# A gated MLP whose down projection is made from seven products of quadrants instead of the plain blocks

## The chip, the core and the metric

One core of a Trainium2 chip runs the whole layer. Its engines run side by side, each with its own instruction queue: TensorE (PE in the profile, with its weight loads shown apart as PEld), VectorE (DVE), ScalarE (ACT), GpSimd (POOL) and SyncE (SP, which here only issues DMAs). The metric is the device time of one execution in microseconds (us); lower is better.

## The reference, cut to what matters

One layer of a causal decoder over 2048 tokens with D = 1024 channels, in float32: attention in eight heads with three dilations beside pooling groups, then a gated MLP of width 2816 with a causal convolution of width 3, then a gated embedding, then a norm.

```python
h = x
hn = _rmsnorm(h, ln_mix[i])
z = hn @ w_in[i]
...
att = _dilated_attention(q, k, v, slopes)
pool = _multiscale_pool(u, pool_w[i], pool_scale[i])
h = h + jnp.concatenate([att, pool], axis=-1) @ w_out[i]
hn = _rmsnorm(h, ln_ffn[i])
up = _causal_dwconv(hn @ w_up[i], conv_w[i], conv_b[i])
gate, val = jnp.split(up, 2, axis=-1)
h = h + (jax.nn.silu(gate) * val) @ w_down[i]
g = jax.nn.sigmoid(_rmsnorm(h, ln_ple[i]) @ w_ple_gate[i])
h = h + g * (p[i] @ w_ple[i])
return _rmsnorm(h, ln_final)
```

The mixture of dilations in the attention weighs each branch by its softmax statistics (`m` the maximum, `d` the denominator): `w = d * exp(m - max(m))`, normalised over the branches.

## The kernel before

**Tiling.** Channels lie on the 128 partitions, tokens on the free axis. A chunk is 512 tokens (`CH`), and there are four (`NCH`). `KD` = 8 blocks of 128 channels make up D, `NF` = 22 blocks the 2816 of the MLP. Every float32 operand of a product is split into a high part (a cast on ACT, L84) and a low part (a subtraction, L85, on DVE or POOL), and `mm3` (L88) multiplies high by high (L89), high by low (L90) and low by high (L91) into the same bank of PSUM: three matmuls of 128x128 by 128x512 for each block.

**Stages.** The input projection runs to about 399 us, the attention to about 735, the output projection `w_out` to about 940, the up product from 942 to 1780 in two halves of 1024 tokens, the down product from 1782 to about 2293, the gate and the final norm to the end.

**Attention.** A list of stages with lags (`CFG["ord"]`) writes out by hand which step of which head each engine does next. `mix` (L705) counts steps d from the end of a pair of heads. At d = 1 the statistics of the pair go to DRAM (tiles std, stf), at 4 they are loaded back (tiles sn and sf), and the list `CFG["m"]` holds the steps of what follows: `mix_lift` (L858: on DVE the minimum `lo` at L862, two differences, an exponential on ACT), `mix_weights` (L870: five operations on DVE and a store of the weights to DRAM by POOL's queue), then for each chunk c `mix_fetch` (the weights broadcast back by POOL's queue), `mix_products` and `mix_store`, both on POOL. Its first three numbers are the step of the lift, of the weights and of the first fetch, the fourth the distance between chunks, the last two the distances from a fetch to its products and its store. Since DVE does its work in the order in which it is written, whatever stands behind L862 waits with it. DVE also does the maxima of the scores (L577, L583), the low part of the transposed weights (L617) and the sum of two halves (L660, once in two steps).

**Up product.** For each of the 22 blocks f and each half there is one turn. A turn computes gate and value block (256 channels by 1024 tokens) with seven products of quadrants in place of eight: the operands a11, a12, a22, s1 to s4 of the activations (`A`, high and low parts of four tiles each) by b11, b21, t2, t1, t3, t4, b22 of the weights (`product`, L1309, 12 matmuls each, L1315). The sums t1 to t4 of the weights are made on POOL in the first half (L1038 to L1040, L1051), stored to DRAM, and loaded back in the second. DVE splits them (L85, tile wu), adds the products (`add`, L1338), does the convolution (`conv_b`, L1328 to L1335) and the product of gate and value (L1512); ACT does the rest (SiLU, L1502). `after(slot)` is called seven times a turn: in turn 0 and around the change of half, `Refill.take` (L1359) splits operands that came by DMA (its `fetch` keeps `depth` loads ahead, in borrowed tiles of the tags nt, inv and dg; low parts at L1372); from turn 2 on, `prepare` (L1097) makes the operands of the second half piece by piece. In it `spread_prep` (L114) makes two diagonal tiles dg for each chunk (L123), and `spread` (L133) broadcasts the scale of a chunk by two matmuls into a bank bc (L137), which frees those tiles. Each turn ends with one store of 128x1024 activations to DRAM (`g.act`, tile act, L1513).

**Down product.** It runs by chunk c, by block f, by eight blocks j of the output: 4 x 22 x 8 x 3 matmuls into seven banks dn and an eighth, dn7, that runs five blocks later (`wait`). `ahead` and `act_ahead` load (SP) and split, three steps ahead, the weights of f (128x1024, tile rd, L954 and L1544) and the activations of f and c (128x512, tile ra, L1559). Three pairs are prepared during the last turn of up (`first_units`, L1379). `closed` adds the residual h (L1586) and stores h2, and `fin` makes the statistics of the norm some steps later. Five of the eight blocks of the gate's weights follow in the same queue of loads behind the last block of down.

The whole of up is written out by hand (`tc.manual_schedule`): its order in the code is its order on every engine. In the down product a scheduler orders each engine's queue.

## Time and profile before

| what | us |
| --- | --- |
| median of 3 runs (2514.61 to 2520.33) | 2520.25 |
| the profiled execution | 2522.12 |
| its span | 2519.8 |
| PE busy | 2407.5 (96%) |
| DVE busy | 1588.8 (63%) |
| ACT busy | 1108.6 (44%) |
| POOL busy | 515.7 (20%) |

The granted clock of PE in this execution is 0.98 on the mean. The chain that ended last lies on PE for 79% of the span, on DMA and on DVE for 6% each. The longest waits of PE by line are:

```profile
PE o L628 <- DVE s L660: 23.3, 30, 4.8
PE o L642 <- DVE s L660: 14.6, 29, 2.5
PE sn L572 <- DVE st L577: 13.6, 3, 6.4
```

A row of the waits names who waited for whom, then us in total, the number of times and the longest. Here all three are in the attention. A row in order of time gives the start, the duration, the engine, the line, the operation, output <- input, shapes, and in brackets the idle time ahead of it with what ended it. A row of groups gives the count, then busy us and mean ns of one, then idle time with what ended it. A row of a stretch gives busy times in the order PE, PEld, DVE, ACT, POOL. Durations of overlapping matmuls are longer than the distance between their starts.

### The profile page before, as it was taken

What the parts mean: (1) busy time and instruction counts of PE and PEld (TensorE: products, weight loads), DVE (VectorE), ACT (ScalarE), POOL (GpSimd) and SP (SyncE); (2) the same over time, 40 slices, a digit from 0 to 9 for tenths busy, and PEclk for the clock granted to TensorE, in tenths of its full rate; (3) what the DMA queues carried; (4) which work ended last, traced back from release to release, by engine and by line L of the source; (5) the groups of instructions that cost most, each with busy time, mean ns of one, the idle gap of its engine ahead of it and who ended that gap; (6) DMA issues with size and microseconds to landing.
All of it is one profiled execution on the core that took longest, in us unless ns stands there. A gap on an engine that the chain in (4) does not pass through costs nothing.

```text
span 2519.8 us, 31897 instructions
## 1 busy us (share of the span) xinstructions
PE 2407.5 (96%) x11515; PEld 2022.4 (80%) x11515; DVE 1588.8 (63%) x2416; ACT 1108.6 (44%) x1923; POOL 515.7 (20%) x423
## 2 busy tenths in 40 slices
PE   8999998888779999999999999999999999999998
PEld 7888887777767877888887888888788888887888
DVE  6635427777774467888888666666535374435755
ACT  5423326887751135544446444444323242323322
POOL 3312221053430023333340000000122222221000
PEclk9999999999879999999999999999999999999999
DMA  7534358687646674555556334333546464635332
GB/s 240 174 120 180 142 178 248 166 193 180 164 164 221 223 252 167 167 177 181 175 194 211 122 117 138 121 114 117 191 134 222 149 219 150 208 122 173 124 105 88
DMA packets 209052, 424.08 MB, mean 168 GB/s; under 512 B 42464, under 2 KB 68896, under 8 KB 205824
## 3 DMA queue, kind: packets, MB, share of 16 engines
q1 hardware_dynamic: 170576, 368.41, 46.4%
q0 software_dynamic: 18672, 25.88, 3.1%
q10 hardware_dynamic: 19648, 27.77, 3.1%
q8 instruction: 90, 1.47, 0.2%
q14 instruction: 66, 0.54, 0.1%
HBM read 290.01 MB, written 131.89 MB: 167 GB/s over the span
## 4 chain that ended last, share of the span: by engine, by line
PE 79%; DMA 6%; DVE 6%; issue 3%; ACT 2%; POOL 0%; SPq 0%; ACTq 0%; POOLq 0%; DVEq 0%
PE ua L1315 18%; PE uc L1315 9%; PE dn L90 6%; PE dn L91 6%; PE dn L89 6%; PE ub L1315 4%; PE z L91 4%; PE z L89 4%; PE z L90 4%; PE o L89 2%; PE o L91 2%; PE o L90 2%; PE gp L89 2%; PE gp L91 2%; PE gp L90 2%
## 5 line engine op out<-in xcount | busy, mean ns | idle before, releaser
L89 PE MATMUL dn<-ah,hd 128*128 128x512 f32 x704 | 275.3, 391 | 2.8 <-ACT ah L84 2.8
L90 PE MATMUL dn<-al,hd 128*128 128x512 f32 x704 | 274.9, 391 | 1.7 <-DVE al L85 1.7
L91 PE MATMUL dn<-ah,ld 128*128 128x512 f32 x704 | 274.6, 390 | 0.0
L85 POOL TENSOR_TENSOR ld<-rd,hd 128x1024 fp32r<-128x1024 f32 x42 | 100.9, 2403 | 812.8 <-ACT hd L84 812.8
L84 ACT CAST hd<-rd 128x1024 fp32r<-128x1024 f32 x88 | 92.5, 1052 | 266.3 <-PE dn L90 230.9
L85 DVE TENSOR_TENSOR al<-ra,ah 128x512 fp32r<-128x512 f32 x88 | 116.8, 1330 | 136.0 <-ACT ah L84 136.0
L89 PE MATMUL z<-hnh,wh 128*128 128x512 f32 (+1 forms) x480 | 170.3, 355 | 9.9 <-ACT hnh L252 5.8
L90 PE MATMUL z<-hnl,wh 128*128 128x512 f32 (+1 forms) x480 | 170.0, 354 | 2.7 <-DVE hnl L253 2.6
L91 PE MATMUL z<-hnh,wl 128*128 128x512 f32 (+1 forms) x480 | 169.9, 354 | 2.3 <-POOL wl L85 1.7
L89 PEld LDWEIGHTS dn<-ah,hd 128*128 128x128 f32 x704 | 132.7, 188 | 31.0 <-ACT ah L84 3.2
L90 PEld LDWEIGHTS dn<-al,hd 128*128 128x128 f32 x704 | 132.7, 188 | 29.8 <-DVE al L85 2.2
L91 PEld LDWEIGHTS dn<-ah,ld 128*128 128x128 f32 x704 | 132.7, 189 | 27.4
L85 DVE TENSOR_TENSOR wu<-ru,wu 128x1024 fp32r<-128x1024 f32 x88 | 127.4, 1448 | 0.0
L155 DVE TENSOR_TENSOR acc<-acc,sq 128x512 f32<-128x512 f32 (+1 forms) x125 | 90.2, 722 | 47.6 <-ACT sq L154 34.6
L1315 PE MATMUL uc<-a22h,wu 128*128 128x512 f32 x352 | 115.7, 389 | 1.8 <-DVE uv L1338 1.8
L1315 PE MATMUL ua<-s2h,wu 128*128 128x512 f32 x352 | 115.8, 390 | 1.1 <-ACT ug L1452 1.1
L1315 PE MATMUL uc<-s3h,wu 128*128 128x512 f32 x352 | 116.2, 390 | 0.3 <-ACT s3h L1371 0.3
L1315 PE MATMUL ub<-a12h,wu 128*128 128x512 f32 x352 | 115.9, 390 | 0.3 <-ACT a12h L1371 0.3
L1315 PE MATMUL ua<-s4h,wu 128*128 128x512 f32 x352 | 115.5, 389 | 0.0
L1315 PE MATMUL ua<-s1h,wu 128*128 128x512 f32 x352 | 115.5, 389 | 0.0
L1315 PE MATMUL ua<-a11h,wu 128*128 128x512 f32 x352 | 115.5, 389 | 0.0
L85 DVE TENSOR_TENSOR ld<-rd,hd 128x1024 fp32r<-128x1024 f32 x46 | 56.2, 1223 | 89.1 <-ACT hd L84 89.1
(317 smaller groups left out, 6474.4 us busy)
## 6 DMA issues: line engine op xcount, KB each, us to landing
rd<-in_w_down_dram SPq DMA_DIRECT2D x88, 512.0 KB, 3.6
ru<-in_w_up_dram SPq DMA_DIRECT2D x66, 512.0 KB, 4.1
ra<-act SPq DMA_DIRECT2D x88, 256.0 KB, 3.8
act<-yg SPq DMA_DIRECT2D x43, 512.0 KB, 3.1
wr<-in_w_in_dram SPq DMA_DIRECT2D x64, 256.0 KB, 4.0
nt<-h SPq DMA_DIRECT2D x56, 256.0 KB, 3.9
h<-h SPq DMA_DIRECT2D x56, 256.0 KB, 5.6
td<-t SPq DMA_DIRECT2D x22, 512.0 KB, 2.6
```

Of the source, the lines that this page charges most:

```text
L84: nc.scalar.copy(hi, src)
L85: (low or nc.gpsimd).tensor_tensor(lo, src, fp(hi), op=ALU.subtract)
L89: nc.tensor.matmul(ps, wh, ah, start=first, stop=False)
L90: nc.tensor.matmul(ps, wh, al, start=False, stop=False)
L91: nc.tensor.matmul(ps, wl, ah, start=False, stop=last)
L155: nc.vector.tensor_tensor(acc[:, :n], acc[:, :n], sq[:, :n], op=ALU.add)
L1315: nc.tensor.matmul(pst, x[:, ksl], y, start=first and k == 0 and n == 0, stop=k == HK - 1 and n == 2, skip_group_check=True)
```

## The change

Four things change together.

1. **Down product.** It works on two halves of 1024 tokens, on pairs of blocks f = q and q + 11, and on quadrants of 128x512. Seven products (`SEQ`) of 11 steps q each go into two groups of four banks, A and B. A product opens a group, or continues it, and the residual h takes a share from four of them. A step loads a weight quadrant `rw` and an activation quadrant `ra`, both 128x512, and DVE makes both low parts.
2. **Activations.** Up goes through its blocks as q, q + 11. It keeps the quadrants a11, a12, a22 as they are, and four sums s1 to s4 are made on DVE after each second turn and stored (`results`, `due_sums`). In the second half, POOL loads the four quadrants of the down weights for each q, makes four differences t1 to t4 and stores them (`down_sums`).
3. **Buffers of up.** The tag nt has five tiles instead of six, `Refill` goes five deep (half 0) and seven deep (half 1) instead of six and ten, and `prepare` starts at turn 3. Five smaller units of the down product are prepared instead of three.
4. **Attention.** The statistics of a pair are used two steps later: lift 9 to 11, weights 10 to 12, fetch 13 to 14, while products (fetch + 5 instead of + 6) and stores stay at the same steps.

```diff
-CFG = {"tt": 2, "ee": 2, 'ord': [['B', 0], ['M', 0], ['N', 0], ['S', 1], ['o', 7], ['F', 0], ['h', 2], ['nm', 0], ['p', 7], ['fm', 0], ['l', 2], ['T', 1], ['V', 6], ['W', 6], ['ne', 0], ['fe', 0]], 'perm': [3, 2, 1, 0], 'fp': [[0], [1], [2], [3]], 'np': [[0, -1], [1], [2], [3]], 'm': [9, 10, 13, 4, 6, 7]}
+CFG = {"tt": 2, "ee": 2, 'ord': [['B', 0], ['M', 0], ['N', 0], ['S', 1], ['o', 7], ['F', 0], ['h', 2], ['nm', 0], ['p', 7], ['fm', 0], ['l', 2], ['T', 1], ['V', 6], ['W', 6], ['ne', 0], ['fe', 0]], 'perm': [3, 2, 1, 0], 'fp': [[0], [1], [2], [3]], 'np': [[0, -1], [1], [2], [3]], 'm': [11, 12, 14, 4, 5, 6]}
...
-def mm3(nc, ps, wh, wl, ah, al, first, last):
-    nc.tensor.matmul(ps, wh, ah, start=first, stop=False)
-    nc.tensor.matmul(ps, wh, al, start=False, stop=False)
-    nc.tensor.matmul(ps, wl, ah, start=False, stop=last)
+def mm3(nc, ps, wh, wl, ah, al, first, last, again=False):
+    nc.tensor.matmul(ps, wh, ah, start=first, stop=False, skip_group_check=again)
+    nc.tensor.matmul(ps, wh, al, start=False, stop=False, skip_group_check=again)
+    nc.tensor.matmul(ps, wl, ah, start=False, stop=last, skip_group_check=again)
...
-        turns = [(half, f) for half in range(2) for f in range(NF)]
+        NP = NF // 2
+        turns = [(half, f) for half in range(2) for q in range(NP) for f in (q, q + NP)]
...
-        FETCH = (("nt", 6), ("inv", 2), ("dg", 2))
+        FETCH = (("nt", 5), ("inv", 2))
...
+            raw = sb.tile([P, 1024], F32, tag="raw", bufs=2, name="rd")[:, :CH]
+            nc.sync.dma_start(raw, w_down[n * P : (n + 1) * P, :CH])
+            tag = ("a11", "s2", "s1")[n // 2]
             ra = opa.tile([P, CH], F32R, tag=tag, bufs=8, name="ra")
-            nc.sync.dma_start(fp(ra), g.act[n][:, :CH])
+            nc.sync.dma_start(fp(ra), g.oq[0]["a11"][n])
...
+        def keep(half, p, q, t):
+            nc.sync.dma_start(g.oq[half][p][q], t)
+
+        sums = []
+
+        def results(pr):
+
+            if pr.f < NP:
+                keep(pr.half, "a11", pr.f, pr.yg[:, lo_])
+                first_f[0] = pr.yg
+                return
+            q, half, one, two = pr.f - NP, pr.half, first_f[0], pr.yg
+            keep(half, "a12", q, two[:, lo_])
+            keep(half, "a22", q, two[:, hi_])
+            x = fp(fb.tile([P, CH], F32R, tag="dg", bufs=2, name="x"))
+
+            def sums_13():
+                nc.vector.tensor_tensor(x, one[:, hi_], two[:, hi_], op=ALU.add)
+                keep(half, "s1", q, x)
+                nc.vector.tensor_tensor(one[:, hi_], one[:, lo_], one[:, hi_], op=ALU.subtract)
+                keep(half, "s3", q, one[:, hi_])
+
+            def sum_2():
+                nc.vector.tensor_tensor(x, x, one[:, lo_], op=ALU.subtract)
+                keep(half, "s2", q, x)
+
+            def sum_4():
+                nc.vector.tensor_tensor(two[:, lo_], two[:, lo_], x, op=ALU.subtract)
+                keep(half, "s4", q, two[:, lo_])
+
+            sums.extend([[0, sums_13], [2, sum_2], [4, sum_4]])
+
+        first_f = [None]
+
+        def due_sums():
+            for e in sums[:]:
+                e[0] -= 1
+                if e[0] < 0:
+                    sums.remove(e)
+                    e[1]()
+
+        def down_sums(q):
+
+            b = []
+            for r in (w_down[q * P : (q + 1) * P, :], w_down[(q + NP) * P : (q + NP + 1) * P, :]):
+                for x in range(2):
+                    t = fb.tile([P, CH], F32, tag="nt", bufs=5, name="nt")
+                    nc.gpsimd.dma_start(t, r[:, x * CH : (x + 1) * CH])
+                    b.append(t)
+
+            def rest():
+                b11, b12, b21, b22 = b
+                for n, (o, x, y) in enumerate(((b11, b12, b11), (b12, b22, b12), (b22, b22, b11), (b21, b21, b22))):
+                    nc.gpsimd.tensor_tensor(o, x, y, op=ALU.subtract)
+                    nc.gpsimd.dma_start(g.dd[q][("t1", "t3", "t2", "t4")[n]], o)
...
-            refill = Refill(0, ("a12", "s3", "a22"), 6)
-            for _ in range(6):
+            refill = Refill(0, ("a12", "s3", "a22"), 5)
+            for _ in range(5):
...
-                    refill = Refill(1, ("a11", "s2", "a12", "s1", "s3", "s4", "a22"), 10)
-                    for _ in range(10):
+                    refill = Refill(1, ("a11", "s2", "a12", "s1", "s3", "s4", "a22"), 7)
+                    for _ in range(7):
...
-                    if 2 <= i < NF - 1 and (7 * i + slot) % 3 == 0 and prep:
+                    if i == 3 and slot == 4:
+                        prep.extend(prepare(1, fb, prep, 5))
+                    if prep and (i == 3 or (i, slot) == (4, 0) or (7 * i + slot) % 3 == 0):
                         prep.pop(0)()
+                    q = i - NF - 2
+                    if 0 <= q < NP and slot == 0:
+                        unit["sum"] = down_sums(q)
+                    if 0 <= q < NP and slot == 2:
+                        unit["sum"]()
+                    due_sums()
...
-                    (nc.gpsimd if over else nc.sync).dma_start(g.act[prev.f][:, prev.half * 1024 : prev.half * 1024 + 1024], prev.yg)
+                    results(prev)
...
+                    unit[4]()
+                    while sums:
+                        due_sums()
...
+        SEQ = (
+            ("a11", "b11", True, True, (0, 0)),
+            ("a12", "b21", False, True, (0, 0)),
+            ("s2", "t2", True, False, (1, 0)),
+            ("s3", "t3", False, True, (1, 1)),
+            ("s1", "t1", True, False, (1, 1)),
+            ("a22", "t4", False, False, (1, 0)),
+            ("s4", "b22", True, False, (0, 1)),
+        )
+        order = [(half, n, q) for half in range(2) for n in range(len(SEQ)) for q in range(NP)]
+
+        def weights(w, q):
+            if w[0] == "t":
+                return g.dd[q][w]
+            r = q + NP * (w[1] == "2")
+            return w_down[r * P : (r + 1) * P, CH * (w[2] == "2") : CH * (w[2] == "2") + CH]
...
+                half, x, q = order[m]
+                rw = fd.tile([P, CH], F32, tag="rw", bufs=4, name="rw")
+                nc.sync.dma_start(rw, weights(SEQ[x][1], q))
+                ra = fd.tile([P, CH], F32, tag="ra", bufs=4, name="ra")
+                nc.sync.dma_start(ra, g.oq[half][SEQ[x][0]][q])
+                w = wtile()
+                split(nc, w[:, :CH], w[:, CH:], rw, nc.vector)
+                ah = fd.tile([P, CH], F32R, tag="ah", bufs=7, name="ah")
+                al = fd.tile([P, CH], F32R, tag="al", bufs=7, name="al")
+                split(nc, ah, al, ra, nc.vector)
+                units[m] = (w[:, :CH], w[:, CH:]), (ah, al)
...
+            pa, wb, chain, starts, (row, col) = SEQ[x]
+            mine = "AB"[(half + (not chain)) % 2]
...
+                if starts:
+                    banks[mine] = [psd.tile([P, CH], F32, tag=mine, bufs=4, name="dn") for _ in range(4)]
+            ahead(n + 4)
+            if n >= len(order) - 8 and n % 2 == len(order) % 2 and len(gates) < NW:
+                gates.append(load_w(rows(w_gate, len(gates)), f"g{len(gates)}", nc.vector))
...
+                mm3(nc, banks[mine][j], wh[:, js], wl[:, js], ah, al, starts and q == 0, q == NP - 1, not starts)
+                if q == NP - 1:
+                    ht = htiles[half, row, col, j]
+                    nc.vector.tensor_tensor(ht, ht, banks[mine][j], op=ALU.add)
+                    if x in (1, 4, 5, 6):
+                        c = 2 * half + row
+                        nc.scalar.dma_start(g.h2[4 * col + j][:, c * CH : (c + 1) * CH], ht)
+                        add_square(nc, fd, acc_of[row], ht, j == 0 and x == (4 if row else 1))
...
+            if half and x == 2 and q in (4, 5):
+                g.pw[q] = rms_scale(nc, g, other("st"), old[q - 4])
+            if half and x == 2 and q == 7:
+                dgs = spread_prep(nc, g, sb, g.pw[4])
+            if half and x == 2 and q == 9:
+                renorm(4, 0, dgs, other)
+            if half and x == 6 and q == 7:
+                g.pw[7] = rms_scale(nc, g, other("st"), acc_of[1])
```

How the order of the instructions moves. On DVE in the attention, where the minimum `lo` of the third pair's statistics is taken (names are tiles; an L583 or L577 with tt is a maximum of the scores, with st alone the reading of its result), before:

```order
L617 TENSOR_TENSOR ptl<-tp,pth 128x512
L862 TENSOR_TENSOR lo<-sn,sf 128x32
L865 TENSOR_TENSOR ex<-lo,sn 128x32
L866 TENSOR_TENSOR ex<-lo,sf 128x32
L577 ISA tt,st_5565<-sn,nb_5117 128x256
```

And now, from behind the same L617 on:

```order
L577 ISA tt,st_5741<-sn,nb_5293 128x256
L577 ISA st_5741 128x1
L583 ISA tt,st_5742<-sf,fb_5294 128x384
L583 ISA st_5742 128x1
L617 TENSOR_TENSOR ptl<-tp,pth 128x384
L577 ISA tt,st_5741<-sn,nb_5293 128x256
L577 ISA st_5741 128x1
L660 TENSOR_TENSOR s_5743<-o,ev 64x512
L583 ISA tt,st_5742<-sf,fb_5294 128x256
L583 ISA st_5742 128x1
L617 TENSOR_TENSOR ptl<-tp,pth 128x768
L862 TENSOR_TENSOR lo<-sn,sf 128x32
```

Two steps of score work, one L660 among them, moved ahead of L862.

On DVE at the end of a turn of up, behind the product of gate and value (yg is that product, wu a low part of weights, yv and uv, ug the convolution's output and inputs), before:

```order
L1512 TENSOR_TENSOR yg<-yg,yv 128x1024
L85 TENSOR_TENSOR wu<-ru_9254,wu 128x1024
L85 TENSOR_TENSOR wu<-t_9388,wu 128x512
L1328 SCALAR_TENSOR_TENSOR yv<-uv,vec,yv 128x1023
L1329 SCALAR_TENSOR_TENSOR yv<-uv,vec,yv 128x1022
L1332 COPY halo<-uv 128x2
L1338 TENSOR_TENSOR ug<-ug,uc 128x512
```

And now, behind each second turn:

```order
L85 TENSOR_TENSOR wu<-t_9864,wu 128x512
L1415 TENSOR_TENSOR x<-yg 128x512
L1417 TENSOR_TENSOR yg<-yg 128x512
L1329 SCALAR_TENSOR_TENSOR yv<-uv,vec,yv 128x1023
L1330 SCALAR_TENSOR_TENSOR yv<-uv,vec,yv 128x1022
L1333 COPY halo<-uv 128x2
L1132 SCALAR_TENSOR_TENSOR nt<-nt,vec,inv 128x512
L1421 TENSOR_TENSOR x<-x,yg 128x512
L1339 TENSOR_TENSOR ug<-ug,uc 128x512
L85 TENSOR_TENSOR wu<-ru,wu 128x1024
L1425 TENSOR_TENSOR yg<-yg,x 128x512
```

The sums s1 (into x) and s3 came in ahead of the convolution, s2 (again into x, L1421) and s4 behind it; L1132 belongs to `prepare` and stands in other turns before.

On SP, where up ends and down begins (oq1 are the stores of the last turn's quadrants and sums, rw and ra the loads of the down product), before:

```order
L1513 DMA act_225<-yg 128x1024
L954 DMA rd_4_15488<-in_w_down_dram 128x1024
L1544 DMA rd<-in_w_down_dram 128x1024 x2
L1559 DMA ra<-act_208 128x512
L1559 DMA ra<-act_209 128x512
```

And now:

```order
L1399 DMA oq1a_303<-yg 128x512
L1399 DMA oq1a_314<-yg 128x512
L1399 DMA oq1s_325<-x 128x512
L1399 DMA oq1s_347<-yg 128x512
L954 DMA rg_19752<-in_w_gate_dram 128x1024
L1399 DMA oq1s_336<-x 128x512
L1399 DMA oq1s_358<-yg 128x512
L1627 DMA rw<-in_w_down_dram 128x512
L1629 DMA ra<-oq0a_210 128x512
```

In place of one store on this queue (that of the very last turn was on POOL's queue before) six now stand ahead of the first loads of the down product's own loop.

More of the change, by code (lines that the diff above doesn't have):

```diff
@@ L1516, in phase_rest @@
                 after(6)
+                if last:
+                    unit[2]()
+                    unit[4] = first_units(4)
+                if over:
+                    unit[4]()
+                    while sums:
+                        due_sums()
                 prev = None if over else cur
@@ L1528, in phase_rest @@
         aux[0] = fd
-        def odd(name):
-            return psd.tile([P, CH], F32, tag="odd", bufs=1, name=name)
-        stat[0] = odd
-        order = [("d", c, f) for c in range(NCH) for f in range(NF)] + [("g", 0, k) for k in range(NW)]
+        SEQ = (
[13 more added lines that the diff above has]
+            return w_down[r * P : (r + 1) * P, CH * (w[2] == "2") : CH * (w[2] == "2") + CH]
         nload = [len(units)]
@@ L1628, in phase_rest, with fin @@
+        def fin(acc=acc_of[0]):
+            g.pw[6] = rms_scale(nc, g, stat[0]("st"), acc)
+        tk.later(6, fin)
+        while len(gates) < NW:
+            gates.append(load_w(rows(w_gate, len(gates)), f"g{len(gates)}", nc.vector))
         dctx.close()
@@ L1635, in phase_rest @@
         aux[0] = db
-        ahead(len(order))
-        wg = [units.pop(("g", 0, k)) for k in range(NW)]
+        wg = gates
         wg += [load_w2(db, rows(w_gate, k), f"wg{k}", nc.vector) for k in range(NW, KD)]
@@ L1799, in tile_layer @@
     g.td = per(NF, [P, S], F32, "td")
-    g.act = per(NF, [P, S], F32, "act")
+    g.oq = [{p: per(NF // 2, [P, CH], F32, f"oq{h}{p}") for p in ("a11", "a12", "a22", "s1", "s2", "s3", "s4")} for h in range(2)]
+    g.dd = [{p: dr.tile([P, CH], F32, tag=f"dd{q}{p}", name=f"dd{q}{p}") for p in ("t1", "t2", "t3", "t4")} for q in range(NF // 2)]
     g.h1 = per(KD, [P, S], F32, "h1")
```

138 lines of the change are left out of this document (47 added, 91 removed).

## The prediction

> **What bounds the kernel now.** I read the busy times of stretches first, then the groups by line, then TensorE (PE) in order of time. Columns of a stretch: its length, busy us (instructions) of PE, PE's weight load, VectorE (DVE), ScalarE (ACT) and GpSimd (POOL), then clock, DMA share, GB/s.
>
> ```profile
> 1246.64:1265.68 19.04, 19.04 (x86) 15.77 (x85) 17.14 (x19) 9.18 (x11) 7.48 (x4) 1.00 0.44 156
> 1589.36:1608.40 19.04, 19.04 (x85) 15.77 (x84) 12.96 (x17) 9.14 (x11) 0.00 (x0) 1.00 0.39 125
> 1790.00:2290.00 500.00, 494.63 (x2180) 408.39 (x2179) 233.53 (x220) 167.46 (x223) 114.75 (x50) 0.99 0.55 181
> ```
>
> The first two rows are one turn of the up product in each half, the third is the down product. PE is busy 19.04 of 19.04 us in a turn and 494.6 of 500 in the down product: there PE alone sets the time, and a thing counts if it removes matmuls or makes PE wait.
>
> ```profile
> L89 PE MATMUL dn<-ah,hd 128*128 128x512 f32 x704 | 275.3, 391 | 2.8 <-ACT ah L84 2.8
> ```
>
> ```profile
> 1782.48 0.39 PE L89 MATMUL dn<-ah,hd 128*128 128x512 f32 x1
> ...
> 1793.36 0.39 PE L89 MATMUL dn<-ah,hd 128*128 128x512 f32 x1
> ```
>
> Matmuls overlap, so the 391 ns of one is not its price. From 1782.48 to 1793.36 us 48 of them start without a gap, so one costs 10.88/48 = **0.2267 us**.
>
> **Fewer matmuls.** The down product has three groups (L89, L90, L91) of 704 = 2112. The changed one has 2 halves x 7 products x 11 steps x 4 banks x 3 = 1848. 264 fewer by 0.2267: **-59.9 us**, all on the path. What could take some back is the change of banks at each of 14 products. A group of banks is used again only after another product of 11 x 12 x 0.2267 = 29.9 us, and four additions on DVE empty it (0.7 each, rows below), so I take nothing and keep +5 (0.4 at each) as the far end: no row shows this change.
>
> **The statistics, two steps later.** DVE reads the statistics of a pair of heads (tile sf) as they land:
>
> ```profile
> 569.22 0.70 DVE L660 TENSOR_TENSOR s<-o,ev 64x512 f32<-64x512 f32 x1
> ...
> 573.56 0.68 DVE L660 TENSOR_TENSOR s<-o,ev 64x512 f32<-64x512 f32 x1 [0.22 <-ACT ev L659]
> ...
> 582.36 0.19 DVE L862 TENSOR_TENSOR lo<-sn,sf 128x32 f32<-128x32 f32 x1 [6.91 <-DMA sf<-stf]
> ...
> 585.50 0.68 DVE L660 TENSOR_TENSOR s<-o,ev 64x512 f32<-64x512 f32 x1
> ...
> 591.41 0.68 DVE L660 TENSOR_TENSOR s<-o,ev 64x512 f32<-64x512 f32 x1
> ...
> 665.04 0.19 DVE L862 TENSOR_TENSOR lo<-sn,sf 128x32 f32<-128x32 f32 x1 [5.95 <-DMA sf<-stf]
> ```
>
> L660 runs once in two steps, so two steps are 4.34 us. DVE, through which every step passes (maxima, low parts, sums), stands still for 6.91 and 5.95 us. In the change two steps of that work stand ahead of the read, as the first listing of DVE in the part on the change shows, while the load is issued where it was. The waits shrink to 2.57 and 1.61: -8.7. Behind the first stall the next two steps took 591.41 - 585.50 = 5.91 instead of 4.34, at a lower clock: twice 1.57 more would go if the clock stayed up. So the gain lies between 8.7 and 11.8. What a shorter pause does to the clock is shown in another place:
>
> ```profile
> 1799.74 0.79 PE L89 MATMUL dn<-ah,hd 128*128 128x512 f32 x1 [2.81 <-ACT ah L84]
> 1802.20 0.80 PE L90 MATMUL dn<-al,hd 128*128 128x512 f32 x1 [1.67 <-DVE al L85]
> ```
>
> After only 2.81 us a matmul takes 0.79 instead of 0.39. So I stay near the lower end: **-9.5**. What follows the read (the weights to DRAM, their fetch, POOL's products) keeps its last step; only POOL waits there.
>
> [...]
>
> **The sums of the activations, on DVE.** Each pair of turns adds four 128x512 operations on DVE; the nearest row is L1338's 0.69.
>
> ```profile
> L1338 DVE TENSOR_TENSOR uv<-uv,uc 128x512 f32<-128x512 f32 x12 | 8.3, 688 | 9.5 <-PE uc L1315 9.5
> L1338 DVE TENSOR_TENSOR ug<-ug,ub 128x512 f32<-128x512 f32 x12 | 8.2, 687 | 19.9 <-PE ub L1315 19.9
> ```
>
> ```profile
> L85 DVE TENSOR_TENSOR wu<-ru,wu 128x1024 fp32r<-128x1024 f32 x24 | 42.4, 1765 | 0.0
> ```
>
> ```profile
> L85 DVE TENSOR_TENSOR wu<-ru,wu 128x1024 fp32r<-128x1024 f32 x25 | 30.5, 1219 | 0.0
> ```
>
> The first three rows are twelve turns of the first half, the last one turns of the second, where POOL stands still. Two sums now come ahead of the convolution of the next turn and two behind it. Four by 0.69 are 2.8 us a pair. DVE's own slack in the first half is what it waits for PE: (9.5 + 19.9)/12 = 2.45 a turn, 4.9 a pair. If both early sums meet POOL's work and grow as L85 does (1765 against 1219: 0.55 more) the cost is 3.9, still below 4.9. The third sum overwrites x while its store may still read it: the wait is new, with the convolution, ug<-ug,uc and all behind it. The convolution covers some 3 us of it, about what a store takes to land (below). I take **+1**, with 0 and +10 (1 us at each of ten pairs) as ends. In the second half 44 new POOL subtractions run beside DVE. L85 and its neighbours made DVE's turn of the first half 17.1 - 13.0 = 4.1 longer with as many, so 13.0 + 1.4 + 4.1 = 18.5, below 19.04: nothing.
>
> [...]
>
> **Start and middle of the up product.**
>
> ```profile
> 996.12 0.69 DVE L123 TENSOR_TENSOR dg<-ident,ph 128x512 fp32r<-128x512 f32 x1 [5.33 <-PE bc L137]
> ...
> 998.07 0.50 PE L1315 MATMUL uc<-a22h,wu 128*128 128x512 f32 x1 [1.75 <-DVE uv L1338]
> ```
>
> ```profile
> 940.38 6.89 DMA nt<-op0s
> ```
>
> ```profile
> 1376.87 0.50 PE L1315 MATMUL ua<-s4l,wu 128*128 128x512 f32 x1 [1.68 <-DVE s4l L1372]
> ```
>
> ```profile
> 1360.88:1379.92 19.04, 17.36 (x77) 14.05 (x76) 18.97 (x28) 14.97 (x25) 0.00 (x0) 1.00 0.74 262
> ```
>
> The second scale waits 5.33 for a buffer that PE's first bc frees, and DVE, late by that, makes PE wait 1.75. The change puts that bc one product (12 matmuls, 2.72 us) earlier: -1.75. But the first loads go five deep instead of six, and the chain of waits shows PE's third operand hanging on a load of 6.89; one load comes about one split (1 us) later: +1. Together **-0.75**, ends -1.75 and +2. At the change of half DVE is full (18.97 of 19.04) and PE waits 1.68 for it. Three or four sums, and seven loads ahead instead of ten, come in there: **+1.5**, ends 0 and +4.
>
> **From up to down.** Before, three prepared units of 21 matmuls (14.3 us) cover the start, then PE idles 2.81 + 1.67 = 4.5.
>
> ```profile
> 1789.12 1.22 DVE L85 TENSOR_TENSOR ld<-rd,hd 128x1024 fp32r<-128x1024 f32 x1
> ...
> 1791.69 0.22 DVE L1335 SCALAR_TENSOR_TENSOR yg<-halo,vec,yg 128x2 f32<-128x2 f32 x1
> ```
>
> ```profile
> 1375.10 1.06 ACT L1502 ACTIVATE yg<-yg 128x1024 f32<-128x1024 f32 x1 [0.92 <-DVE halo L1332]
> ```
>
> ```profile
> 1379.13 1.22 DVE L1512 TENSOR_TENSOR yg<-yg,yv 128x1024 f32<-128x1024 f32 x1
> ```
>
> ```profile
> L84 ACT CAST ah<-ra 128x512 fp32r<-128x512 f32 x88 | 53.7, 615 | 13.5 <-DMA ra<-act 13.5
> ```
>
> ```profile
> ra<-act SPq DMA_DIRECT2D x88, 256.0 KB, 3.8
> ```
>
> ```profile
> act<-yg SPq DMA_DIRECT2D x43, 512.0 KB, 3.1
> ```
>
> Now five units of 12 stand ready, and the loads of the sixth are issued behind all six stores of the last turn (the listing of SP there). That turn's convolution ended at 1791.9; 1.1 sooner without the weight split (1.22, overlapping by 0.1) that stood in it, 1790.8. Then SiLU 1.1 and the product 1.2: 1793.1. Two sums: 1794.5. x stored and landed, 3.1: 1797.6. Two more sums: 1799.0, and only then the last store and the loads: 3.8 and a cast of 0.6: 1803.4. The units end at 1782.48 + 60 x 0.2267 = 1796.1, with some 1.7 of waiting for the fifth 1797.8. Idle 5.6 + 1.7 = 7.3 against 4.5: **+3** with the clock, ends 0 (the stores land sooner) and +8 (two units late).
>
> **From down to gate.**
>
> ```profile
> 2290.00:2305.00 15.00, 11.45 (x42) 8.35 (x41) 5.60 (x6) 5.53 (x6) 2.13 (x2) 0.89 0.92 314
> ```
>
> 42 matmuls stand where 66 fit: 24 x 0.2267 = 5.4 us lost, while the last weights come through two buffers. Now five gate weights are loaded and split in the last eight steps of down and right behind it, some 10 us sooner than before: **-4.5**, with a wait of about 1 us left; ends -5.4 and 0.
>
> **Sum:** -59.9 - 9.5 + 1 - 0.75 + 1.5 + 3 - 4.5 = -69.15. The profiled execution took 2522.12 us (span 2519.8): 2453.0. It lies 1.87 above the median of the runs, 2520.25, so 2451.1, say **2451**. Against the median, all good ends together give 2441.4 and all bad ones 2480.5.
>
> **Rivals.**
>
> ```profile
> L1040 POOL TENSOR_TENSOR ru<-ru,t 128x512 f32<-128x512 f32 x22 | 45.3, 2058 | 1.7
> ```
>
> (1) Each new POOL subtraction blocks DVE for most of its length, some 1.9 us: 13.0 + 1.4 + 4 x 1.9 = 22.0 a turn, 3.0 over PE's, in 11 turns +33: **2484**. For it speaks L1040, which takes 2058 ns for what DVE does in 0.69; against it the growth of L85, 0.55. Chance 0.11.
>
> (2) The statistics' step does not do what it says: the steps moved ahead of the read bring their own transfers, which stand in the queue with sf, and sf lands later by as much. The 9.5 stay: **2460**. A landing at 582, two steps behind its reader, speaks for a queue that is full; its unmoved issue speaks against. 0.10.
>
> (3) **Slower than before:** the down product becomes fed by DMA. A step now needs 512 KB in 2.72 us, 193 GB/s, and with 64 tiles h of 256 KB read and written over 419 us some 230, against 181 now. Four buffers are under way, so a round trip may take 10.9 us; now it would be 3.8 + 2 x 0.62 + 2 x 0.69 = 6.4. From 12.7 on (a step of 3.17, over 154 steps 69 us) all is lost. At a landing of 11 it is 13.6, a step of 3.4, +105: **2556**. The 314 GB/s of the stretch from 2290 show that the engines can carry it: 0.04.
>
> **Chances.** The forecast has 0.75, the rivals 0.11, 0.10 and 0.04. The range 2440 to 2480 takes in all ends of the unknown costs and (2), and leaves out (1) and (3). 0.3%, 7.6 us, is about what a measurement tells from no change. Only (3) is slower, and only a sum of (1) with all bad ends comes near no change: faster 0.94, same 0.02, slower 0.04.
>
> **What would show it.** Right: 1848 dn matmuls at 0.2267 and a down stretch near 419 us; waits for sf near 2.6 and 1.6; turns of 19.04 with PE full in both halves; one pause of about 7 us some 14 us into down; no pause at the first gp. Turns longer than 19.04 with DVE full would be rival 1, waits for sf as long as before rival 2, down steps over 2.8 us with waits for rw or ra rival 3. A term off by more than its ends would make the prediction wrong; the likeliest is the way from up to down, where six stores, four sums and two pools of buffers meet.

## The result, and the profile after

The changed kernel takes **2551.85 us** (median of 4 runs, 2545.99 to 2561.60) against 2519.66 before: a ratio of 1.0131, interval 1.0105 to 1.0156. It is slower by 1.3% where 2451 was forecast.

Where the time went is read from the first matmul of each stage, that of the attention from the last matmul of the input projection, in the two profiled executions (2519.8 and 2548.0 us of span):

| stage | before, us | after, us | difference | predicted |
| --- | --- | --- | --- | --- |
| input projection | 397.5 | 396.9 | -0.6 | 0 |
| attention | 336.3 | 417.7 | **+81.4** | -9.5 |
| output projection | 196.9 | 197.1 | +0.2 | 0 |
| up | 851.8 | 863.2 | **+11.4** | +1.75 |
| down | 490.4 | 432.6 | -57.8 | -56.9 |
| gate and final norm | 246.9 | 240.5 | -6.4 | -4.5 |
| sum | 2519.8 | 2548.0 | +28.2 | -69.15 |

The down product, the reason for all the rest, came out as worked out. In order of time on PE, the two pauses of the changed kernel at its start:

```profile
1887.96 0.50 PE L90 MATMUL dn<-al,wu 128*128 128x512 f32 x1 [1.75 <-DVE al L85]
1895.68 0.80 PE L89 MATMUL dn<-ah,wu 128*128 128x512 f32 x1 [4.93 <-ACT ah L84]
```

They are 1.75 and 4.93 us long; 1.7 and 5.6 were forecast. Behind them PE has no gap, and none stands between down and gate (busy times, columns as in the prediction):

```profile
2000.00:2250.00 250.00, 250.00 (x1112) 207.22 (x1111) 158.12 (x254) 119.78 (x211) 2.19 (x2) 1.00 0.72 227
```

```profile
2305.00:2320.00 15.00, 15.00 (x67) 12.40 (x67) 10.02 (x13) 6.97 (x10) 3.41 (x2) 1.00 0.74 259
```

The attention is another picture. The same 40 us of it, before and then after:

```profile
560.00:600.00 40.00, 27.31 (x152) 24.82 (x153) 23.72 (x74) 24.93 (x68) 12.24 (x14) 0.83 0.71 158
```

```profile
560.00:600.00 40.00, 9.90 (x52) 9.18 (x52) 7.64 (x22) 9.76 (x26) 14.53 (x15) 0.68 0.60 150
```

PE, DVE and ACT are all busy for less than half as long, while POOL is busy for longer. The waits of the changed kernel over its whole span, first of PE, then of DVE and of POOL (who <- whom: us in total, times, longest):

```profile
PE o L628 <- DVE s L660: 93.2, 31, 32.7
PE tp L600 <- DVE nr L806: 25.3, 1, 25.3
```

```profile
DVE s L660 <- POOL m L902: 62.3, 2, 32.4
DVE nr L806 <- POOL m L908: 23.7, 1, 23.7
```

```profile
POOL wb L891 <- issue: 168.5, 19, 21.5
```

PE waits for DVE, DVE waits for POOL, and POOL waits for nothing that the profile can name, 19 times, each time at the issue of a broadcast wb (`mix_fetch`, L891). DVE's second wait stands at the end of the attention: there the tile nr takes over a buffer of POOL's products (tag m3), and POOL is late with the pair before. With 62.3 it makes 86.0 us, where DVE waited in the attention before 12.9 for sf and for POOL not at all. POOL's row reads before:

```profile
POOL wb L891 <- issue: 23.2, 3, 11.7
```

In order of time on POOL, the first broadcasts of a pair before, and then after:

```profile
502.03 0.77 POOL L880 DMA_DIRECT2D wd<-wts  x1 [100.30 <-DVE st L577]
504.49 2.43 POOL L891 DMA_DIRECT2D wb<-wd  x3 [1.70 <-DMA wd<-wts]
512.95 0.79 POOL L891 DMA_DIRECT2D wb<-wd  x1 [6.03 <-DMA wb<-wd]
```

```profile
507.40 0.84 POOL L891 DMA_DIRECT2D wb<-wd  x1 [1.91 <-DMA wd<-wts]
515.21 0.81 POOL L891 DMA_DIRECT2D wb<-wd  x1 [6.98 <-issue]
537.48 0.80 POOL L891 DMA_DIRECT2D wb<-wd  x1 [21.46 <-issue]
546.74 0.79 POOL L891 DMA_DIRECT2D wb<-wd  x1 [8.47 <-issue]
```

Before, three broadcasts leave one behind the other and the fourth waits. After, they leave one by one; a broadcast lands 7.5 us after its issue in the median, 22.0 at the longest. The diff has another line, not shown above, which halves a size in bytes:

```diff
-    nc = bacc.Bacc("TRN2", target_bir_lowering=False, num_devices=1, dynamic_dma_scratch_size=4096)
+    nc = bacc.Bacc("TRN2", target_bir_lowering=False, num_devices=1, dynamic_dma_scratch_size=2048)
```

Below it is called the room. The expectations call it the room for GpSimd's descriptors, which is the author's reading: what is kept in it no run shows, only what follows from its size. That gives two theories of the 81 us. **Theory 1**: the room is too small, POOL's queue becomes serial, and POOL's products of one pair still read the tile s when DVE wants to write it for a later pair. **Theory 2**: the moved steps (lift two later, fetch to products 5 instead of 6) leave POOL too little time.

### The profile page after: what moved, and what is told of

Its sections match the earlier page's. It is cut to its first block, busy times and chain, and to the rows that moved or that the text cites. A ratio compares the mean times of both kernels' runs of the same rounds, so it can differ in the third digit from the quotient of the medians.

```text
span 2548.0 us, 32497 instructions
## 1 busy us (share of the span) xinstructions
PE 2355.6 (92%) x11251; PEld 1979.5 (78%) x11251; DVE 1724.8 (68%) x2705; ACT 1147.6 (45%) x2055; POOL 523.9 (21%) x509
## 4 chain that ended last, share of the span: by engine, by line
PE 64%; issue 15%; DVE 9%; POOL 4%; DMA 3%; ACT 1%; SPq 0%; POOLq 0%; DVEq 0%; ACTq 0%
PE ua L1316 13%; PE uc L1316 7%; PE dn L89 5%; PE dn L90 5%; PE dn L91 5%; PE ub L1316 4%; PE z L91 4%; PE z L89 4%; PE z L90 4%; DVE wu L85 2%; PE o L91 2%; PE o L89 2%; PE gp L89 2%; PE o L90 2%; PE gp L91 2%
## 5 line engine op out<-in xcount | busy, mean ns | idle before, releaser
L89 PE MATMUL dn<-ah,wu 128*128 128x512 f32 x616 | 241.4, 392 | 4.9 <-ACT ah L84 4.9
L90 PE MATMUL dn<-al,wu 128*128 128x512 f32 x616 | 241.0, 391 | 1.7 <-DVE al L85 1.7
L91 PE MATMUL dn<-ah,wu 128*128 128x512 f32 x616 | 240.7, 391 | 0.0
L110 POOL TENSOR_TENSOR pw<-ms,mhalf 128x4 f32<-128x4 f32 (+1 forms) x18 | 17.9, 996 | 887.7 <-ACT ms L108 878.3
L85 DVE TENSOR_TENSOR al<-ra,ah 128x512 fp32r<-128x512 f32 x154 | 105.9, 690 | 109.6 <-ACT ah L84 108.0
L84 ACT CAST ah<-ra 128x512 fp32r<-128x512 f32 x154 | 95.3, 621 | 146.9 <-PE dn L91 133.7
L89 PEld LDWEIGHTS dn<-ah,wu 128*128 128x128 f32 x616 | 116.3, 189 | 29.3 <-ACT ah L84 5.4
L90 PEld LDWEIGHTS dn<-al,wu 128*128 128x128 f32 x616 | 116.3, 189 | 26.9 <-DVE al L85 2.6
L628 PE MATMUL o<-pth,v 128*128 128x256 f32 (+1 forms) x152 | 49.2, 344 | 93.2 <-DVE s L660 93.2
L91 PEld LDWEIGHTS dn<-ah,wu 128*128 128x128 f32 x616 | 116.3, 189 | 24.2
L85 DVE TENSOR_TENSOR wu<-rw,wu 128x512 fp32r<-128x512 f32 x149 | 101.0, 687 | 23.1 <-ACT wu L84 21.8
L600 PE MATMUL tp<-ident,ee 128*128 128x128 f32 x568 | 90.7, 290 | 27.5 <-DVE nr L806 25.3
```

The source lines that it names most:

```text
L84: nc.scalar.copy(hi, src)
L85: (low or nc.gpsimd).tensor_tensor(lo, src, fp(hi), op=ALU.subtract)
L89: nc.tensor.matmul(ps, wh, ah, start=first, stop=False, skip_group_check=again)
L90: nc.tensor.matmul(ps, wh, al, start=False, stop=False, skip_group_check=again)
L91: nc.tensor.matmul(ps, wl, ah, start=False, stop=last, skip_group_check=again)
L110: nc.gpsimd.tensor_tensor(pw[:, :nj], ms[:, :nj], g.mhalf[:, :nj], op=ALU.pow)
```

## The experiments

Ratios are to the kernel before, measured on the same chip (2523.56, 2522.35 and 2521.11 us in the three groups of four). Of long lines an edit shows only the part that changes.

### The room alone, and the steps alone

`b_scratch`, the kernel before with one number:

```diff
-dynamic_dma_scratch_size=4096
+dynamic_dma_scratch_size=2048
```

> The kernel before, with nothing changed but the room for GpSimd's DMA descriptors, 2048 bytes instead of 4096. Theory 1 (the room holds one broadcast wb at a time instead of three, POOL waits at each issue, DVE waits for POOL): the attention grows by 70 to 90 us, the broadcasts are issued singly with 5 to 20 us between them, 2590 to 2610 us. Theory 2 (the moved steps of the statistics leave POOL too little time): no change, 2515 to 2525 us.

Measured: **2605.28 us**, 1.0338 (1.0312 to 1.0364). The attention takes 420.0 us, every other stage what it took before to within 3 us. Its waits:

```profile
POOL wb L891 <- issue: 183.1, 18, 25.8
```

```profile
DVE s L660 <- POOL m L902: 69.8, 2, 37.8
```

The room alone makes the whole loss of the attention, in a kernel that has nothing else of the change.

`b_steps`, the kernel before with the six numbers:

```diff
-'m': [9, 10, 13, 4, 6, 7]
+'m': [11, 12, 14, 4, 5, 6]
```

> The kernel before with the six numbers of the statistics' steps alone changed, room 4096 as before. Theory 1: the waits for sf shrink to 2.6 and 1.6 as predicted and the time to 2508 to 2512 us; broadcasts still go out three at once. Theory 2: POOL falls behind by the step, DVE waits for POOL as in the changed kernel, 2590 to 2600 us.

Measured: 2525.45 us, 1.0015 (0.9998 to 1.0032). Theory 2 falls: nothing like 80 us. But the gain of 9.5 us isn't there either. The waits for sf are gone, not only shorter, and in their place stands, in order of time on DVE and then on POOL:

```profile
584.43 0.68 DVE L660 TENSOR_TENSOR s<-o,ev 64x512 f32<-64x512 f32 x1 [9.35 <-POOL m L902]
```

```profile
573.73 1.29 POOL L901 TENSOR_TENSOR m<-s,wb 128x512 f32<-128x512 f32 x1 [14.29 <-DMA wb<-wd]
582.88 1.51 POOL L902 TENSOR_TENSOR m<-s,wb 128x512 f32<-128x512 f32 x1 [7.87 <-DMA wb<-wd]
```

POOL's chain for the pair (weights, broadcasts, four products) begins 4.5 us later (506.49 against 502.03 us), and its last product ends at 584.4 instead of 561.1, since its last broadcasts, issued at 550 us, stand among the loads of the next heads (v, ks, qhh, qll on SP from 547 to 570) and land only at 573 and 582. DVE then waits 14.1 us in two places for POOL, where it waited 12.9 for sf. The attention is 340.9 us against 336.3.

### The change with the old steps, and with a little more room

`a_oldsteps`, the changed kernel with `'m': [9, 10, 13, 4, 6, 7]`:

> The changed kernel with the old six numbers of the steps, room still 2048. Theory 1: still slow, 2540 to 2570 us, the attention about 80 us longer than before. Theory 2: the 81 us of the attention go, 2465 to 2475 us.

Measured: 2549.95 us, 1.0103 (1.0070 to 1.0135), attention 416.0 us. As theory 1 has it.

`a_2560`, the changed kernel with

```diff
-dynamic_dma_scratch_size=2048
+dynamic_dma_scratch_size=2560
```

> The changed kernel with room 2560 instead of 2048. Theory 1: three broadcasts fitted 4096 and one 2048, so two should fit here if one takes at most 1280 bytes; then more than half of the 81 us go, 2465 to 2510 us; if one takes more, nothing changes. Theory 2: 2545 to 2560 us.

Measured: **2482.49 us**, 0.9850 (0.9826 to 0.9874). 512 bytes are worth 69 us. On POOL in order of time two broadcasts now leave together:

```profile
511.68 1.63 POOL L891 DMA_DIRECT2D wb<-wd  x2 [1.84 <-DMA wd<-wts]
521.47 0.79 POOL L891 DMA_DIRECT2D wb<-wd  x1 [8.16 <-issue]
```

The attention is 354.2 us, still 18 above that of before, with DVE waiting 19.9 us for POOL.

### The broadcasts on another queue

`a_wbsp`, room 2048:

```diff
-                        mix_fetch(nc, g, mx, nc.gpsimd, pr, pairs[pr], c)
+                        mix_fetch(nc, g, mx, nc.sync, pr, pairs[pr], c)
```

> The changed kernel, room still 2048, with the broadcasts wb issued on SP's queue instead of GpSimd's. If the room for GpSimd's descriptors is what costs (theory 1), GpSimd no longer waits at its issues, DVE's waits for m L902 go, the attention is back at 327 to 341 us (418 now) and the time at 2460 to 2475 us. If instead the broadcasts themselves are late, whatever queue they take (theory 2: too few steps between fetch and products), DVE still waits tens of us for m L902: 2530 to 2555 us.

Measured: 2520.27 us, 0.9997 (0.9985 to 1.0010): between the two. POOL's waits at issues are gone and DVE's for m L902 too, as theory 1 says, but the attention is 389.2 us, not 341. Waits of SP's queue that the kernel before does not have say why:

```profile
SPq L891 <- DMA wd<-wts: 38.0, 3, 15.6
SPq L891 <- POOL m L901: 32.4, 6, 6.4
SPq L56 <- DMA wb<-wd: 31.6, 6, 10.8
SPq L891 <- POOL m L902: 20.5, 4, 5.6
```

A broadcast now waits there for the weights (38 us in three places) and for POOL to free its tile, and the loads of the next heads (L56) stand behind it: PE waits 29.5 us for ks, where it waited 1.0 before. The issue itself is slow there, too. Its row gives the shortest, median and longest in ns, then the first and last start in us, first on POOL in the kernel before, then on SP:

```profile
L891 POOL DMA_DIRECT2D wb<-wd x24: 792/830/859, 504.5 to 698.3; - x24
```

```profile
L891 SPq DMA_DIRECT2D wb<-wd x24: 484/4896/7128, 509.8 to 745.2; - x24
```

One wait was exchanged for another.

### The 11 us of the up product

The distance between the first matmuls of successive turns is 19.04 us where nothing is lost. What lies above it, by place, in us of one profiled execution each (all other turns are at 19.04; `a_4096` and below are described in the next part). The two turns at the change of half are the first two of the second half; GpSimd's sums run from the second of them to the tenth or eleventh turn of that half, and the last column counts from the third turn on:

| kernel | first five turns | the two turns at the change of half | turns with GpSimd's sums |
| --- | --- | --- | --- |
| before | 8.9 | 2.4 | 0 |
| after | 8.4 | 7.7 | 6.7 |
| a_oldsteps | 6.0 | 5.6 | 9.4 |
| a_2560 | 6.1 | 7.4 | 5.3 |
| a_wbsp | 7.4 | 5.6 | 7.5 |
| a_spread | 6.6 | 6.1 | 5.6 |
| a_x2 | 7.2 | 5.2 | 2.4 |
| a_lowpool | 5.8 | 6.4 | 6.8 |
| a_4096 | 7.5 | 5.8 | 8.7 |
| a_4096_old | 7.7 | 7.6 | 5.6 |
| a_best | 9.9 | 5.7 | 1.5 |
| a_nosub | 9.1 | 4.3 | 0 |

Profiles with the same code in a place scatter by several us, so only a difference beyond that scatter tells anything.

Three edits, each on top of room 2560. `a_spread` writes the weight sums of the down product into every second turn:

```diff
-                    q = i - NF - 2
+                    q = {2 * n + NF + 2 - (n == NP - 1): n for n in range(NP)}.get(i, -1)
```

> Room 2560, and the weight sums of the down product on GpSimd in every second turn of the second half instead of in every one of its first eleven. Theory A (the 5.3 us that these turns lose come from DVE running full while GpSimd works): a turn without them gives DVE time, the loss falls below 2 us, 2477 to 2481 us. Theory B (each meeting costs PE its own time): 22 turns share the same 5.3 us, 2482 us as with room 2560 alone.

Measured: 2484.00 us, 0.9850 (0.9829 to 0.9871), 5.6 us lost, as theory B has it. But the trace shows that the edit moved nothing. GpSimd's 44 subtractions in `a_2560`, then in `a_spread`, in rows of the same kind as above:

```profile
L1451 POOL TENSOR_TENSOR nt<-nt x44: 1269/1346/1978, 1400.2 to 1565.7; 128x512 f32<-128x512 f32 x44
```

```profile
L1451 POOL TENSOR_TENSOR nt<-nt x44: 1278/1351/2044, 1397.3 to 1564.9; 128x512 f32<-128x512 f32 x44
```

POOL has no other work there. It waits once for the tiles that it borrows and then for its own loads alone (45.6 us in `a_spread`), so it does the sums as early as before, within nine turns, in whatever turn they are written. Neither theory was tested.

`a_x2` gives s2 a tile of its own:

```diff
+            y = []
...
+                y[:] = [fp(fb.tile([P, CH], F32R, tag="dg", bufs=2, name="x2"))]
-                nc.vector.tensor_tensor(x, x, one[:, lo_], op=ALU.subtract)
-                keep(half, "s2", q, x)
+                nc.vector.tensor_tensor(y[0], x, one[:, lo_], op=ALU.subtract)
+                keep(half, "s2", q, y[0])
...
-                nc.vector.tensor_tensor(two[:, lo_], two[:, lo_], x, op=ALU.subtract)
+                nc.vector.tensor_tensor(two[:, lo_], two[:, lo_], y[0], op=ALU.subtract)
```

> Room 2560, and s2 written to a tile of its own instead of over x, so that DVE no longer waits for the store of s1. Theory A (that wait, 9.7 us of DVE in the turns with GpSimd's sums, is what makes those turns longer): their 5.3 us go, the half change loses 1 to 2 less, 2475 to 2478 us. Theory B (DVE is full through its slower operations there, 18.5 of 19.04, and the wait is hidden): at most 1 us, 2481 to 2483 us.

Measured: 2479.15 us, 0.9829 (0.9803 to 0.9855). The interval overlaps that of `a_2560`, but the turns with GpSimd moved: they lose 2.4, where the eight profiles without this tile lose 5.3 to 9.4. At the change of half 5.2 lies just below the 5.6 to 7.7 of the profiles with the same code there, which one profile can't tell apart. The wait for the store is a part of the loss, not all of it.

`a_lowpool` makes every third low part at the change of half on POOL (nine of 28):

```diff
-                    nc.vector.tensor_tensor(lo, t, fp(hi), op=ALU.subtract)
+                    (nc.gpsimd if self.half and m % 3 == 1 else nc.vector).tensor_tensor(lo, t, fp(hi), op=ALU.subtract)
```

> Room 2560, and at the change of half every third low part of the operands on GpSimd, which stands still there, instead of on DVE (9 of 28, 6 us of DVE). Theory A (the two turns at the change lose 7.4 us because DVE is full): they lose 2 to 4, 2478 to 2480 us. Theory B (they lose it because loads come late, seven deep instead of ten): no change, 2482 us; GpSimd's slower subtractions could even hold PE up, 2484.

Measured: 2481.54 us, 0.9839 (0.9818 to 0.9861): no gain. It doesn't tell the theories apart. PE then waited 3.4 us for a low part s4l of DVE, where it waited 1.9 in `a_2560`, and DVE was not relieved in the first turn of the second half: busy for 24.43 of its 24.58 us with 27 operations, against 21.64 of 22.20 with 31.

### The full room, and what is then left

In `a_4096` the room is 4096 again; the 2 KB come from the tile t4, which takes a tile that lies idle during up:

```diff
-fb.tile([P, CH], F32, tag="t4", name="t4")
+sb.tile([P, CH], F32, tag="acc", bufs=1, name="t4")
-dynamic_dma_scratch_size=2048
+dynamic_dma_scratch_size=4096
```

> The changed kernel with room 4096, as before the change; the 2 KB come from the tile t4, which borrows a tile that lies idle during up. Theory 1 (the room alone made the attention long): three broadcasts go out at once again, the attention is 341 us as with the steps alone, 13 less than at room 2560, and the time 2466 to 2471 us. If something else of the change takes part in the attention's 81 us: above 2475 us.

Measured: **2467.00 us**, 0.9800 (0.9774 to 0.9826), 84.9 us below the changed kernel (medians on different chips, where the kernel before differs by 1.5). In order of time on POOL, three at once again:

```profile
506.18 2.42 POOL L891 DMA_DIRECT2D wb<-wd  x3 [1.70 <-DMA wd<-wts]
514.22 0.78 POOL L891 DMA_DIRECT2D wb<-wd  x1 [5.62 <-DMA wb<-wd]
```

The attention took 331.1 us in this execution, 5 less than before, with no wait for POOL and none for sf; in `a_nosub`, whose attention is the same code, it took 345.6 with one wait of 12.2 for POOL. So a single profile tells of these collisions only to some 10 us.

`a_4096_old` has the old six numbers besides.

> As a_4096, with the old six numbers of the steps. If the moved steps only put a wait for GpSimd in the place of the wait for sf: attention 336 us, the waits for sf 6 to 7 us each again, 2462 to 2468 us, up to 5 below a_4096. If the moved steps gain what was predicted once the room is there: 2475 to 2480 us.

Measured: 2462.54 us, 0.9775 (0.9750 to 0.9801). The old steps are 4.5 us better here and 1.9 in the kernel before (`b_steps`); each interval overlaps. The moved steps gain nothing that can be measured.

`a_best` adds to `a_4096_old` the tile of its own for s2, and writes GpSimd's sums two turns later:

```diff
-                    q = i - NF - 2
+                    q = i - NF - 4
```

> As a_4096_old, with s2 in a tile of its own and the weight sums on GpSimd beginning two turns later, so that none falls into the change of half. Theory (DVE is full at the change and its operations grow beside GpSimd; the wait for s1's store adds to it): the half change loses 5 instead of 7, the turns with GpSimd 2 instead of 5; 2458 to 2462 us. If the losses are DMA's: 2463 to 2468 us, as a_4096_old.

Measured: **2461.55 us**, 0.9770 (0.9751 to 0.9788), the fastest median of all, 59.6 us below the kernel before, though not to be told from `a_4096_old`. The turns with GpSimd lose 1.5 us, and since `a_x2` has the tile without the later place, the tile is what both have. The later place moved nothing here either: the first subtraction still starts 17.6 us ahead of the third turn of the second half, as in `a_4096` (17.5). So the 5.7 at the change of half don't tell what GpSimd's sums cost there.

`a_nosub` tells what in those turns costs. It lacks one line of `a_4096`, without which the result is no longer that of the layer:

```diff
-                    nc.gpsimd.tensor_tensor(o, x, y, op=ALU.subtract)
```

> As a_4096, but GpSimd's 44 subtractions of the down product's weights are left out (the tiles are loaded and stored unchanged). If the subtractions hold DVE up (its operations grow from 1.22 to 1.8 beside them): the turns with them go to 19.04, 4 to 6 us less than a_4096. If the loads and stores do it (the wait for s1's store, 250 GB/s): the loss stays within 1 us of a_4096's.

Measured: 2466.10 us, 0.9777 (0.9741 to 0.9812); the time is uncertain by more than the question, the trace is not. All its turns behind the change of half take 19.04 us, with GpSimd's loads and stores in them. The ten turns from the third of the second half on, busy times in `a_4096` and then in `a_nosub`:

```profile
1394.15:1593.23 199.08, 193.70 (x842) 158.35 (x841) 177.97 (x182) 90.66 (x111) 101.13 (x116) 0.99 0.71 245
```

```profile
1411.96:1602.36 190.40, 190.40 (x841) 157.71 (x840) 142.03 (x182) 91.48 (x111) 38.56 (x71) 1.00 0.72 250
```

The DMAs move about as much (245 and 250 GB/s), but for the same 182 operations DVE is busy for 178.0 us with the subtractions and 142.0 without. In the same stretches, groups of DVE, `a_4096` and then `a_nosub`:

```profile
L85 DVE TENSOR_TENSOR wu<-ru,wu 128x1024 fp32r<-128x1024 f32 x21 | 30.8, 1467 | 0.0
...
L1421 DVE TENSOR_TENSOR x<-x,yg 128x512 f32<-128x512 f32 x5 | 4.9, 983 | 10.4 <-DMA oq1s<-x 10.4
```

```profile
L85 DVE TENSOR_TENSOR wu<-ru,wu 128x1024 fp32r<-128x1024 f32 x21 | 25.6, 1218 | 0.0
...
L1421 DVE TENSOR_TENSOR x<-x,yg 128x512 f32<-128x512 f32 x5 | 3.5, 692 | 18.1 <-DMA oq1s<-x 18.1
```

Without the subtractions DVE's operations have the length that they have where POOL stands still (1219 ns for wu), and DVE then waits even longer for the store of s1, 18.1 us, at no cost to PE. With `a_x2` and `a_best` this says that the slower operations alone (2.4 and 1.5 us lost) and the wait alone (none lost) are each nearly bearable; together they make DVE late (5.3 to 9.4).

## Why the prediction was wrong

**The step that failed is one that the prediction doesn't have.** Of the change it says which instructions go, come and move; the room is no instruction, and it got no term, no rival and no place in the diff as it was shown. The prediction's sentence on what follows the statistics ("What follows the read (the weights to DRAM, their fetch, POOL's products) keeps its last step; only POOL waits there") takes it for granted that POOL can issue when it comes to an issue. With half the room it can't (168.5 us of idle time at its issues, 23.2 before), and POOL's lateness, which the sentence leaves with POOL, reaches DVE through the tiles s and nr and PE through DVE: b_scratch +81.7, the changed kernel against a_4096 +84.9, the changed kernel with old steps against a_4096_old +87.4 us. Without it, the change is worth -54.1 us (a_4096 against 2521.11) where -69.15 was forecast. Its 2467.00 would lie inside the range of 2440 to 2480, but not for the reasons given: the statistics gain nothing and up loses more, as told below.

The trace of before had the clue. Its second pair of heads issues three broadcasts and then this row:

```profile
596.16 0.79 POOL L891 DMA_DIRECT2D wb<-wd  x1 [5.42 <-issue]
```

An idle 5.42 us on POOL that nothing releases, right behind three DMAs of its own queue: beside the runs above it reads as a room of 4096 that was already full. A change that halves it could have been priced from there: a broadcast lands in 7.5 us at the least in that trace, and eight for each of three pairs, one at a time, are some 180 us of POOL as an estimate. 168.5 came.

**The fewer matmuls** were right: -57.8 with the way into down, -56.9 forecast. The bank changes cost nothing (PE is busy for 250.00 of 250.00 us above). The pauses at the start of down came within 0.7 us, and none is left at the gate (-6.4, of -4.5).

**The statistics** were wrong as a mechanism. The wait for sf does go, but what was called harmless, POOL's chain beginning later, ends at DVE (14.1 us of waiting in `b_steps`): the tile s is read by POOL's products. The rivals had the wait stay, none had it replaced. It is worth 0 with an uncertainty of some 5 us, where -9.5 was forecast. (All bad ends together give 2480.7, not 2480.5.)

**The sums of the activations**: the first half was right. From the sixth turn on its turns stay at 19.04 us in the profile (DVE busy 16.2 to 19.0 of them), and a stretch of that length without POOL grew on DVE by the sums' 1.2 us, from 12.96:

```profile
1706.40:1725.44 19.04, 19.04 (x86) 15.77 (x85) 14.16 (x18) 9.15 (x11) 0.00 (x0) 1.00 0.44 143
```

In the second half beside POOL, 18.5 of 19.04 was forecast for DVE. The eight turns from the third of that half on, and the last two of them:

```profile
1484.67:1642.00 157.33, 154.37 (x673) 125.61 (x672) 143.60 (x138) 70.16 (x85) 100.89 (x116) 1.00 0.78 265
```

```profile
1601.22:1621.76 20.54, 19.63 (x85) 15.61 (x84) 20.21 (x22) 11.35 (x14) 14.48 (x15) 1.00 0.68 233
1621.76:1642.00 20.24, 19.33 (x85) 15.69 (x84) 14.82 (x15) 6.81 (x9) 11.74 (x15) 1.00 0.81 269
```

On the mean DVE is busy for 143.60/8 = 17.95 us a turn, so the sum was about right. The "nothing" drawn from it was not, since the load is uneven: DVE is full in one turn (20.21 of 20.54) and stands in the next for the store of s1:

```profile
1635.11 0.69 DVE L1421 TENSOR_TENSOR x<-x,yg 128x512 f32<-128x512 f32 x1 [5.32 <-DMA oq1s<-x]
```

At 18.5 of 19.04 there is no slack for a wait of 5 us, and 6.7 us were lost. Nor does POOL keep to four subtractions a turn, as the forecast has it: behind the wait for its borrowed tiles little but its own loads paces it (49.2 us of waiting), and it does its 44 within nine turns instead of eleven. That POOL's subtractions hold DVE up is what the first rival supposed; they do, at a fifth of its price, and by what means no run shows. DVE's extra 35.9 us beside 40 subtractions (`a_4096` against `a_nosub`) are 0.90 us for each, about three fifths of what one takes on POOL (1.48), where the rival had nearly all of its 2.06 and the forecast 0.55 for a meeting.

**The start** of up was right as far as profiles can tell: 8.4 us lost instead of 8.9, and 5.8 to 9.9 in the eleven profiles with the changed start. **The change of half** was mis-sized: +5.3 for +1.5, and +3.2 at the least in the profiles with the same code there. DVE has next to no free time in these two turns (busy for 44.53 of 45.76 us), so the four sums (2.7 us) may come through whole, which no run shows; what the rest is made of stays open, since a_lowpool could not relieve DVE there.

**The third rival**, the only one on the slower side, did not occur: behind its first 21 us down never waits for data (PE is busy for 404.00 of the 404.00 us from 1896 to 2300). The result is slower by another way.

## What to carry to other kernels

Read the parts of a diff that issue nothing (sizes of rooms, depths, launch options) as carefully as the instructions. Here one of them set how many broadcasts leave at once (three with 4096, two with 2560, one with 2048), and an idle time that nothing releases, 5.42 us right behind DMAs of the engine's own, was the sign that no fourth could. Where a change makes a wait disappear, ask what the next reader of the same tile does; here, in `b_steps`, DVE waited for POOL as long as it had for the load (14.1 us against 12.9). An engine forecast at 97% of a turn is not free: a long wait that it must also take (5.32 us of DVE in one turn here) can come out at the bound. And look in the trace whether an edit moved what it was meant to move: POOL, paced by little but its own loads, did not keep to the turns in which its 44 subtractions are written (nine turns in `a_2560` and in `a_spread` alike).

## What was not expected of the hardware

The cost is a staircase in the room. Three broadcasts of 256 KB leave at once with 4096 bytes, two with 2560 and one with 2048. If each takes the same share, that share, as an estimate from these three runs, is more than 1024 bytes and at most 1280. With 2048 GpSimd, issuing one at a time, pays the landing of each, 7.5 us in the median of the changed kernel. The engine stands still at the issue (168.5 us in the changed kernel, 183.1 in `b_scratch`), and the profile names nobody for it.
